# Tile 7's depthwise taps for both token chunks on TensorE, and one modulation section moved from TensorE to VectorE

## The chip, the cores and the metric

The kernel runs on one core of a Trainium2 chip. The metric is device microseconds of one execution. Before the change the median of three runs is 1677.97 us (1677.6 to 1678.09).

## The reference

A trunk of two layers over 1024 tokens of 1024 channels. Each layer is RMSNorm, shift and scale from a conditioning vector, a token mixer, a gated residual add, and then the same with a SwiGLU feed-forward part. The change concerns the first layer: its mixer (`conformer_conv`) and its modulation vector.

```python
def reference(x, c, ...):
    c_act = jax.nn.silu(c)
    for i in range(DEPTH):
        mod = c_act @ ada_w[i] + ada_b[i]
        sh_m, sc_m, g_m, sh_f, sc_f, g_f = jnp.split(mod, N_ADA, axis=-1)
        h = modulate(rms_norm(x, norm_mix_g[i]), sh_m, sc_m)
        ...
        x = x + (1.0 + g_m)[:, None, :] * y
        h = modulate(rms_norm(x, norm_ffn_g[i]), sh_f, sc_f)
        y = swiglu_ffn(h, ffn_w_gate[i], ffn_w_up[i], ffn_w_down[i])
        x = x + (1.0 + g_f)[:, None, :] * y

def conformer_conv(h, w1, b1, w_dw, b_dw, ln_g, ln_b, w2, b2):
    u = h @ w1 + b1
    a, g = jnp.split(u, 2, axis=-1)
    u = a * jax.nn.sigmoid(g)
    u = lax.conv_general_dilated(u, w_dw[:, None, :], ...,     # causal, depthwise,
        padding=[(CONV_WIDTH - 1, 0)], ...) + b_dw             # CONV_WIDTH = 31 taps
    u = jax.nn.silu(layer_norm(u, ln_g, ln_b))
    return u @ w2 + b2
```

## The kernel before

Channels lie on the 128 partitions in 8 tiles (0 to 7), tokens on the free axis in two chunks of 512, called A and B. Engines are named PE (TensorE), DVE (VectorE), ACT (ScalarE), POOL (GpSimd) and SP (SyncE) as in the profile. float32 products are made of three matmuls of split operands (high by high, high by low, low by high; `products`): a weight `w` has a high and a low part, and so have the activations. Low parts of weights are made by DVE, or by a DMA that adds the raw weight onto the negated high part (issued by POOL, `w<-in_..._dram`).

The instruction stream is written by a planner. Work for PE stands in a list of units; between matmuls `pace()` lets a set of tasks (generators) issue a step for DVE, ACT or POOL when the planner's clocks say so. A task that reaches a `yield "name"` is held for the time that the table `DELAY` gives that name. So the costs and delays, not the code's order alone, set where a vector instruction or a small matmul stands on its engine. Each engine then runs its instructions in the order written.

The stages that matter here, in order of PE's work in the first layer:

- `conv_in`: for each chunk and tile, 24 matmuls into bank `a` and 24 into bank `g` (weights w1, inputs `h`); `conv_glu` then makes u = (a + b1) * sigmoid(g + b1) on ACT and DVE. A rim of 30 tokens (`uhalo`) carries A's last tokens over to B.
- The 31 taps of the convolution. For most tiles class `Taps` makes them: DVE steps `ca<-u,vecs,ca` (a scalar times a shifted u plus a running sum, 128x512), and for a part of the taps ACT products `pr` that POOL adds up (`pa<-pa,pr`); then `ca<-pa,ca` joins the two and `u<-u,vecs,ca` ends the tile. For A's tile 6 (15 taps) and A's tile 7 (all 31) PE makes taps: `pe_taps` multiplies shifted windows of u (high and low part, `us`) by diagonal 128x128 matrices of tap weights (`wdg`), and the bank `tap` collects them. Tile 7 of A is 31 taps by 3 matmuls, with 512 columns at the first tap and down to 482 at the last.
- `layer_norm_silu(A)`: DVE adds the eight tiles into `acc`, a matmul with `ones` makes the mean (`mean<-acc,ones`), DVE subtracts it (`u<-u,mean`), then come squares, `var<-ones,acc`, `rstd<-ident,col`, and the normalised values `v`. PE fills the time with `conv_in` of B's tiles 3, 4 and 5.
- `conv_out(A)`: eight output tiles `y<-v,w` of 24 matmuls; then the last `conv_in` of B (tile 5), beside which the feed-forward norm of A (`norm_a`: `var`, `rstd`) runs; then the feed-forward part for A (`p<-h,w` for gate and up, `dn<-g,w` for down), beside which DVE and POOL finish B's taps and `layer_norm_silu(B)` runs.

The modulation vector has six sections of 1024 numbers (j = 0 to 5). In the first layer j = 0 and 1 are made by DVE dot products (`ada_dot`: weights `adaw` times the activated c, with the sum written to `mod`). j = 2 to 5 are made by PE in `ada_columns`: 32 matmuls `ada<-adaw,ccols` of 32 by 256 for a section, issued in pairs of two k (8 matmuls), then two `adac<-quarters,t` and a DVE add `mod<-adac,vecs`. j = 5 is the gate of the feed-forward residual, used first when A's `dn` ends. The weights `adaw` come through SP's queue into two buffers.

Of the kernel before, what the change touches and what calls it, by code (L numbers as in the profile page):

```python
# [133 lines left out]
def trunk(ctx, tc, xT, c, vec, ada, adan, w1f, w1, wdg, w2, wgu, wdn, wds, wpl, out):  # L134
# [267 lines left out]
    def ada_task(l, js, pause=None, first=None):  # L402

        def gen():
            todo = [(j, k) for j in js for k in range(KT)]
            ws = [ada_load(ada[(l * 6 + j) * KT + k], soft) for j, k in todo[:ADA_BUFS]]
# [333 lines left out]
    def conv_glu(ch, p, ba, bg, own=False):  # L740
# [5 lines left out]
        if ch.i == 0 and PE_TAPS.get(p) == CW:  # L746

            V_.scalar_tensor_tensor(ba, ba, V("conv_b1", p), sg, op0=ADD, op1=MUL)
            pair = wpair(B, "us", F32R)
            hi, lo = st["us", p] = [pair[:, i, : ch.width] for i in range(2)]  # L750
            for part in (hi, lo):
                G_.memset(part[:, HALO - 2 : HALO].bitcast(F32), 0.0)
            S_.copy(hi[:, HALO:], ba)
            V_.tensor_tensor(lo[:, HALO:], ba, hi[:, HALO:].bitcast(F32), op=SUB)
            S_.copy(uhalo[:, p, :], ba[:, ch.n - HALO :])
            return
# [42 lines left out]
    def pe_taps(p):  # L799
# [4 lines left out]
        for i, js in enumerate(groups):  # L804
            def emit(take, i=i, js=js):
# [3 lines left out]
                for q, j in enumerate(js):  # L809
                    full = PE_TAPS[p] == CW  # L810
                    o = (CW - 1 - j) // 2 * 2 if full else CW - 3 - j
                    c = j + o if full else 0
                    products(b[:, o:], wt, q, [v[:, c : c + A.n - o] for v in st["us", p]], j == groups[0][0], j == groups[-1][-1])
                    if q % 4 == 3:
                        pace()
                if i == len(groups) - 1:
                    if full:
                        S_.activation(st["u", 0, p][:, HALO:], b, AF.Identity, bias=V("conv_bdw", p))
                        st["taps", 0][p] = True
                    else:  # L820
                        T["taps", 0, p].other = b
# [1435 lines left out]
```

## Time and profile before

| | |
|---|---|
| median of three runs | 1677.97 us |
| profiled execution | 1675.66 us, span 1673.9 us, granted clock 0.998 |
| PE busy | 1651.8 us, 99% of the span |
| DVE busy | 1310.0 us, 78% |
| ACT busy | 804.1 us, 48% |
| POOL busy | 487.4 us, 29% |

The span is the time from the first to the last instruction of the profiled execution; 1.8 us lie around it. PE's share of 99% is one over the whole program. In the table below, of stretches in us from the span's start, the columns are the time and the number of instructions in which each engine was busy (PEld is the loading of weights, which overlaps PE), PE's granted clock, the mean share of the 16 DMA engines and GB/s. The change touches the first four stretches.

```profile
60.00:180.00 120.00, 119.71 (x610) 89.84 (x610) 107.87 (x169) 96.16 (x138) 90.41 (x84) 1.00 0.78 225
180.00:240.00 60.00, 60.00 (x306) 47.65 (x305) 52.17 (x86) 45.71 (x62) 43.76 (x41) 1.00 0.91 228
240.00:320.00 80.00, 79.95 (x415) 62.70 (x414) 72.90 (x115) 63.03 (x89) 59.71 (x53) 1.00 0.79 213
320.00:420.00 100.00, 98.69 (x433) 80.17 (x432) 90.88 (x120) 70.40 (x103) 80.54 (x61) 1.00 0.59 174
420.00:1674.00 1254.00, 1244.80 (x5607) 1033.39 (x5605) 933.02 (x1298) 505.68 (x671) 189.53 (x286) 1.00 0.74 228
```

### The profile page before, as it was taken

The page shows a single profiled execution, that of the slowest core. Times are in us where ns is not written, and L with a number is a line of the kernel's source. Part 1 is how long each engine was busy: PE and PEld are TensorE (multiplying, and loading weights), DVE is VectorE, ACT ScalarE, POOL GpSimd, SP SyncE. Part 2 cuts the span into 40 slices and gives each one's busy share as a digit, 9 for nine tenths or more (in the row PEclk, how much of TensorE's full clock was granted, in tenths as well). Part 3 has the DMA queues.
Part 4 walks back from the last instruction along what each step waited for, and adds up shares of the span by engine and source line. Part 5 has one row for each costly group of instructions (what it writes and reads, how often), then busy time and mean ns, then how long its engine had stood idle before and what let it go on. Part 6 is the DMA issues. An engine that isn't in the chain of part 4 may idle for free.

```text
span 1673.9 us, 21194 instructions
## 1 busy us (share of the span) xinstructions
PE 1651.8 (99%) x7550; PEld 1351.2 (81%) x7550; DVE 1310.0 (78%) x1867; ACT 804.1 (48%) x1090; POOL 487.4 (29%) x567
## 2 busy tenths in 40 slices
PE   7999999999999999999999999999999999999997
PEld 5777878787888888888888888888888888888887
DVE  8889899799759888888678957848777766658657
ACT  3669696867546332332234436637322222244354
POOL 3587777796002111221100502101111111000013
PEclk9999999999999999999999999999999999999999
DMA  8958997828776888886965959866777776686664
GB/s 301 295 176 228 225 236 205 226 78 241 229 234 168 278 264 287 282 272 206 400 231 164 285 155 283 247 211 199 189 225 222 220 227 183 207 273 207 192 170 126
DMA packets 117180, 378.60 MB, mean 226 GB/s; under 512 B 12369, under 2 KB 14545, under 8 KB 117074
## 3 DMA queue, kind: packets, MB, share of 16 engines
q1 hardware_dynamic: 79664, 245.63, 41.6%
q0 software_dynamic: 36832, 131.09, 32.5%
q8 instruction: 59, 0.97, 0.2%
q10 hardware_dynamic: 578, 0.53, 0.1%
q14 instruction: 47, 0.39, 0.1%
HBM read 310.61 MB, written 62.39 MB: 223 GB/s over the span
## 4 chain that ended last, share of the span: by engine, by line
PE 88%; POOL 3%; DVE 2%; DMA 2%; issue 2%; ACT 2%; DVEq 0%; SPq 0%; POOLq 0%; ACTq 0%
PE a L151 24%; PE dn L151 23%; PE e L151 14%; PE p L151 10%; PE y L151 6%; POOL pa L128 3%; PE first L151 3%; PE g L151 2%; PE tap L151 2%; DMA adaw<-in_adan_dram 1%; DMA s<-in_wds_dram 1%; PE ada L151 1%; ACT w L128 1%; DMA w<-in_wgu_dram 1%; PE var L151 1%
## 5 line engine op out<-in xcount | busy, mean ns | idle before, releaser
L128 ACT CAST w<-raw 128x1024 fp32r<-128x1024 f32 (+1 forms) x247 | 254.6, 1033 | 305.5 <-PE dn L151 56.9
L128 DVE TENSOR_TENSOR w<-raw,w 128x1024 fp32r<-128x1024 f32 (+1 forms) x173 | 209.3, 1214 | 62.2 <-ACT w L128 61.9
L151 PE MATMUL a<-n,w 128*128 128x512 f32 x1056 | 246.8, 389 | 0.2
L151 PE MATMUL p<-h,w 128*128 128x512 f32 x1056 | 243.7, 390 | 1.2 <-DMA w<-in_wgu_dram 1.0
L128 POOL TENSOR_TENSOR pa<-pa,pr 128x512 f32<-128x512 f32 x159 | 225.3, 1500 | 29.0 <-ACT pr L128 23.7
L151 PEld LDWEIGHTS p<-h,w 128*128 128x128 f32 x1056 | 197.3, 188 | 43.7 <-DMA w<-in_wgu_dram 1.4
L151 PEld LDWEIGHTS a<-n,w 128*128 128x128 f32 x1056 | 198.0, 188 | 42.2 <-DVE r L128 1.1
L151 PE MATMUL dn<-hi,w 128*128 128x512 f32 (+1 forms) x768 | 226.2, 377 | 0.4 <-DVE w L128 0.4
L151 PE MATMUL dn<-g,w 128*128 128x512 f32 x864 | 199.1, 390 | 0.2 <-DVE x L128 0.2
L151 PEld LDWEIGHTS dn<-g,w 128*128 128x128 f32 x864 | 161.7, 188 | 34.7 <-DVE x L128 0.6
L128 DVE SCALAR_TENSOR_TENSOR ca<-u,vecs,ca 128x512 f32<-128x512 f32 x246 | 170.6, 747 | 0.5
L151 PEld LDWEIGHTS dn<-hi,w 128*128 128x128 f32 x768 | 141.2, 188 | 27.0 <-DVE w L128 0.9
L151 PE MATMUL dn<-lo,w 128*128 128x512 f32 (+1 forms) x384 | 144.3, 376 | 0.0
L151 PE MATMUL a<-t,w 128*128 128x512 f32 x528 | 123.3, 389 | 0.0
L151 PE MATMUL e<-t,w 128*128 128x512 f32 x528 | 123.3, 389 | 0.0
L151 PE MATMUL e<-b,w 128*128 128x512 f32 x528 | 123.3, 389 | 0.0
L128 ACT ACTIVATE pr<-u,vecs 128x512 f32<-128x512 f32 x159 | 108.4, 717 | 25.0 <-POOL pa L128 19.7
L151 PEld LDWEIGHTS a<-t,w 128*128 128x128 f32 x528 | 99.1, 188 | 20.7
L151 PEld LDWEIGHTS e<-t,w 128*128 128x128 f32 x528 | 99.1, 188 | 20.6
L151 PEld LDWEIGHTS e<-b,w 128*128 128x128 f32 x528 | 99.1, 188 | 20.6
L1191 POOL DMA_DIRECT2D raw<-in_wgu_dram x41 | 36.5, 889 | 271.5 <-DVE r L128 104.2
L128 ACT CAST hi<-op 128x1024 fp32r<-128x1024 f32 (+1 forms) x52 | 48.5, 935 | 87.1 <-PE dn L151 77.2
(191 smaller groups left out, 2449.4 us busy)
## 6 DMA issues: line engine op xcount, KB each, us to landing
raw<-in_wgu_dram SPq DMA_DIRECT2D x132, 512.0 KB, 4.7
raw<-in_wds_dram SPq DMA_DIRECT2D x48, 512.0 KB, 6.0
adaw<-in_ada_dram POOLq DMA_DIRECT2D x48, 512.0 KB, 6.8
kinds<-k POOLq DMA_DIRECT2D x42, 512.0 KB, 7.7
raw<-in_wgu_dram POOLq DMA_DIRECT2D x41, 512.0 KB, 7.3
raw<-in_w_dram SPq DMA_DIRECT2D x36, 512.0 KB, 6.6
op<-kinds SPq DMA_DIRECT2D x36, 512.0 KB, 4.8
adaw<-in_adan_dram SPq DMA_DIRECT2D x32, 512.0 KB, 5.5
```

What stands on the lines that cost most here:

```text
L128: self.last = self.order(getattr(self.eng, name)(out, *args, **kw))
L151: last_mm[0] = nc.tensor.matmul(out, lhsT, rhs, start=start, stop=stop, skip_group_check=more).ins.name
L1191: d = order(nc.gpsimd.dma_start(w[i], wgu[l, fp, src], accum_op=ADD))
```

## The change

1. Tile 7's taps are made on PE for both chunks. Tokens are split into even and odd ones (two phases, f), and the 128 rows of a matrix are 2 phases by 64 channels, for each half g of the tile's channels. A matmul then carries 512 columns: 256 token pairs of A beside 256 of B. 31 taps become 16 pair shifts m, so that 2 halves by 16 shifts by 3 products give 96 matmuls of 512 columns, with matrices that couple the two phases (`dense`), in place of 93 for A alone. `halves` makes the operands (four DVE steps of 64x256 for each chunk, a high copy on ACT and a low part on DVE), and ACT brings the result back in eight pieces of 64x256. DVE's and POOL's 31 taps for B's tile 7 are gone.
2. j = 5 of the first layer is made by `ada_task` on DVE (eight dot products of 128x1024, sum and gain on POOL) in place of `ada_columns`. Its weights come through SP's queue as before, from another array; it is created after j = 4 is done (`scale_done`) and ended in `first_head`.
3. `conv_out(A)` makes its output tiles 0 and 1 in turn (k by k), as B's did.
4. The mean of A's layer norm is delayed by 4.6 of the planner's us ("mean") in place of 2.75 ("stats").

```diff
-DELAY = {"stats": 2.75, "spread": 3.0, ...
+DELAY = {"mean": 4.6, "stats": 2.75, "spread": 3.0, ...
-    def ada_task(l, js, pause=None, first=None):
+    def ada_task(l, js, pause=None, first=None, queue=soft):
...
+        if PE_TAPS.get(p) == CW:
+            return u
...
+    def halves(ch, p, ba, sg):
+
+        n = ch.n // 2
+        t = temp(ch.n).rearrange("p (g n) -> p g n", g=2)
+        for g in range(2):
+            at = slice(HALF * g, HALF * g + HALF)
+            for f in range(2):
+                V_.scalar_tensor_tensor(t[HALF * f : HALF * f + HALF, g], ba[at].rearrange("p (n f) -> p f n", f=2)[:, f], V("conv_b1", p)[at],
+                                        sg[at].rearrange("p (n f) -> p f n", f=2)[:, f], op0=ADD, op1=MUL)
...
+        S_.copy(hi, t)
+        V_.tensor_tensor(lo, t, hi.bitcast(F32), op=SUB)
+
+    def pe_halves(p):
+
+        blocks = [(g, m) for g in range(2) for m in range(NM)]
...
+                    products(b, wt, q, [part[:, g, m : m + 512] for part in st["us", p]], m == 0, m == NM - 1)
...
+                            for f in range(2):
+                                at = slice(HALF * f, HALF * f + HALF)
+                                S_.activation(d[:, f], b[at, n * ch.i : n * ch.i + n], AF.Identity, bias=V("bdw_halves", g)[at])
...
-        yield "soon" if ch.i else "stats"
+        yield "soon" if ch.i else "mean"
...
-        for ds in [(0, 1) if ch.i else (0,), *(() if ch.i else ((1,),)), *((d,) for d in range(2, KT))]:
+        for ds in [(0, 1), *((d,) for d in range(2, KT))]:
...
-        for u in pe_taps(p):
+        for u in pe_halves(p) if PE_TAPS[p] == CW else pe_taps(p):
             unit(*u)
...
-        T["ada_f"] = Task(ada_columns((4, 5)), False, 0)
+        T["ada_f"] = Task(ada_columns((4,)), False, 0)
...
-    taps(B, *some, *rest[: len(rest) - HOLD - HOLD_LN])
+    taps(B, *[p for p in some if PE_TAPS.get(p, 0) < CW], *rest[: len(rest) - HOLD - HOLD_LN])
...
     unit(scale_done)
+    unit(lambda take: T.__setitem__("ada_g", ada_task(0, (5,), "load", queue=sync)))
...
-        unit(lambda take: finish(T["ada_f"]))
+        unit(lambda take: finish(T["ada_g"]))
```

How the order changes, at three places. Rows are instructions in the order of an engine, with the numbers of the tiles; "x3" is three in a row.

First place: DVE between the add `mod<-adac,vecs` of section j = 3 (it waits for two small matmuls of PE that stand behind the first 12 tap matmuls of tile 7) and the first `ca<-pa,ca` behind it; both kernels then go on to the last add of A's `acc`, which the mean waits for. Before:

```order
L128 TENSOR_TENSOR mod<-adac_1792,vecs 128x8
L128 SCALAR_TENSOR_TENSOR ca_1559<-u_721,vecs,ca_1559 128x512
L128 SCALAR_TENSOR_TENSOR ca_1591<-u_721,vecs,ca_1591 128x512
...
L128 TENSOR_TENSOR ca_1559<-pa_1529,ca_1559 128x512
L128 SCALAR_TENSOR_TENSOR ca_1591<-u_721,vecs,ca_1591 128x512
L128 SCALAR_TENSOR_TENSOR u_721<-u_721,vecs,ca_1559 128x512
```

After:

```order
L130 TENSOR_TENSOR mod<-adac_1796,vecs 128x8
L130 SCALAR_TENSOR_TENSOR ca_1622<-u_721,vecs,ca_1622 128x512
L130 SCALAR_TENSOR_TENSOR ca_1566<-u_721,vecs,ca_1566 128x512
...
L130 TENSOR_TENSOR ca_1566<-pa_1556,ca_1566 128x512
L130 SCALAR_TENSOR_TENSOR ca_1622<-u_721,vecs,ca_1622 128x512
L130 SCALAR_TENSOR_TENSOR u_721<-u_721,vecs,ca_1566 128x512
```

The rows left out are `ca` steps of the same two running sums: between `mod` and the first `ca<-pa,ca` stand 6 of them before and 17 after. Up to the mean's last `acc` it is 33 DVE instructions before and 41 after, the difference being 8 `ca` steps.

Second place: PE at the end of the tap matmuls. Before:

```order
L151 MATMUL tap_1779<-us_1229,w_1735 128x484 x6
L151 MATMUL tap_1779<-us_1229,w_1735 128x482 x3
L151 MATMUL a_1975<-h_801,w_1769 128x512 x3
...
L151 MATMUL a_1975<-h_808,w_1769 128x512 x3
L151 MATMUL mean_2010<-acc_1962,ones 128x512
L151 MATMUL g_1976<-h_801,w_1829 128x512 x3
```

After:

```order
L153 MATMUL tap_1889<-us_1233,w_1742 128x512
L153 MATMUL tap_1889<-us_1232,w_1742 128x512
L153 MATMUL a_1996<-h_801,w_1776 128x512 x3
...
L153 MATMUL a_1996<-h_808,w_1776 128x512 x3
L153 MATMUL mean_2031<-acc_1983,ones 128x512
L153 MATMUL g_1997<-h_801,w_1834 128x512 x3
```

The mean stands behind the same 24 matmuls of `conv_in` as before; the taps ahead of it are 512 wide throughout.

Third place: PE around the mean of B's layer norm, in the feed-forward part. Before:

```order
L151 MATMUL dn_3976<-g_3744,w_3796 128x512 x3
L151 MATMUL dn_3977<-g_3744,w_3796 128x512 x3
L151 MATMUL mean_3990<-acc_3961,ones 128x512
L151 MATMUL dn_3974<-g_3843,w_3848 128x512 x3
L151 MATMUL dn_3975<-g_3843,w_3848 128x512 x3
```

After:

```order
L153 MATMUL p_3718<-h_2812,w_3663 128x512 x3
L153 MATMUL p_3718<-h_2813,w_3663 128x512 x3
L153 MATMUL mean_3861<-acc_3841,ones 128x512
L153 MATMUL p_3719<-h_2810,w_3663 128x512 x3
L153 MATMUL p_3719<-h_2811,w_3663 128x512 x3
```

Before, the mean stands behind 12 matmuls of the down projection; after, it stands 36 matmuls ahead of that projection's start, which is 48 matmuls earlier. From B's layer norm on, the order of all engines soon becomes the same in both kernels.

More of the change, by code (lines that the diff above doesn't have):

```diff
@@ L104, in tap_groups @@
     n = PE_TAPS[p]
-    todo = list(range(CW - 1, -1, -1) if n == CW else range(CW - 3, CW - 3 - 2 * n, -2))
+    todo = list(range(CW - 3, CW - 3 - 2 * n, -2))
     return [todo[i : i + DIAGS] for i in range(0, len(todo), DIAGS)]
@@ L400, in ada_load @@
         return w
[L402 removed]
+    def ada_task(l, js, pause=None, first=None, queue=soft):
         def gen():
             todo = [(j, k) for j in js for k in range(KT)]
[L406 removed]
+            ws = [ada_load(ada[(l * 6 + j) * KT + k], queue) for j, k in todo[:ADA_BUFS]]
             for i, (j, k) in enumerate(todo):
@@ L411, in gen @@
                     j2, k2 = todo[i + ADA_BUFS]
-                    ws.append(ada_load(ada[(l * 6 + j2) * KT + k2], soft))
+                    ws.append(ada_load(ada[(l * 6 + j2) * KT + k2], queue))
                 if k == KT - 1:
@@ L745, in conv_glu @@
             tc.add_manual_dep(S_.last.ins, st.pop("v_high"), edge, reason="behind the layer norm's last high part")
[L746 to L755, printed above, removed]
+        if PE_TAPS.get(p) == CW:
+            halves(ch, p, ba, sg)
             return
@@ L809, in emit @@
                 for q, j in enumerate(js):
[L810 to L813, printed above, removed]
+                    o = CW - 3 - j
+                    products(b[:, o:], wt, q, [v[:, : A.n - o] for v in st["us", p]], j == groups[0][0], j == groups[-1][-1])
                     if q % 4 == 3:
@@ L816, in emit @@
                 if i == len(groups) - 1:
[L817 to L821, printed above, removed]
+                    T["taps", 0, p].other = b
             us.append((emit, wdg[sum(len(tap_groups(q)) for q in PE_TAPS if q < p) + i]))
@@ L2207 @@
         ada_b, norm_mix_g, norm_ffn_g, conv_b1, conv_bdw, conv_ln_g, conv_ln_b, conv_b2, c, pool_ls, final_g, conv_wdw)])
+    whole = [p for p in PE_TAPS if PE_TAPS[p] == CW]
+    vec = np.concatenate([vec, np.tile(np.asarray(conv_bdw).reshape(KT, 2, HALF)[whole].reshape(-1, HALF), (1, 2))])
     def tiles(w, f):
@@ L2219 @@
     taps = np.asarray(conv_wdw)[0].reshape(CW, KT, P)
-    groups = [(p, js) for p in sorted(PE_TAPS) for js in tap_groups(p)]
+    groups = [(p, js) for p in sorted(PE_TAPS) if PE_TAPS[p] < CW for js in tap_groups(p)]
     diag = np.zeros((len(groups), P, DIAGS, P), np.float32)
@@ L2224 @@
             diag[i, range(P), q, range(P)] = taps[j, p]
+    dense = np.zeros((len(whole), 2, NM, 2, HALF, 2, HALF), np.float32)
+    for i, p in enumerate(whole):
+        for m in range(NM):
+            for f in range(2):
+                for o in range(2):
+                    j = 2 * (m - LEAD) + CW - 1 + f - o
+                    if 0 <= j < CW:
+                        dense[i, :, m, f, range(HALF), o, range(HALF)] = taps[j, p].reshape(2, HALF).T
+    dense = dense.reshape(-1, DIAGS, P, P).transpose(0, 2, 1, 3)
+    diag = np.concatenate([diag, dense])
     down = np.asarray(ffn_w_down).reshape(DEPTH, NP, 2, P, 2, D // 2)
```

32 lines of the change are left out of this document (29 added, 3 removed).

## The prediction

> **What bounds the kernel now.** I read the busy times first, then the chain that ended last, then what TensorE (PE) waited for, and then the timeline of PE and DVE in the stretches that the change touches.
>
> From the page: busy times, and shares of the chain by engine.
>
> ```profile
> PE 1651.8 (99%) x7550; PEld 1351.2 (81%) x7550; DVE 1310.0 (78%) x1867; ACT 804.1 (48%) x1090; POOL 487.4 (29%) x567
> PE 88%; POOL 3%; DVE 2%; DMA 2%; issue 2%; ACT 2%; DVEq 0%; SPq 0%; POOLq 0%; ACTq 0%
> ```
>
> PE's waits (line, releaser: total us, times, longest):
>
> ```profile
> PE var L151 <- DVE acc L128: 4.9, 1, 4.9
> ...
> PE p L151 <- DMA w<-in_wgu_dram: 1.0, 1, 1.0
> ```
>
> PE is busy for 99% of the span and carries 88% of the chain. The largest wait, 4.9 us, belongs to the first norm of the program. In the stretches of the change only the 1.0 us for `w<-in_wgu_dram` is a wait of size. So the time is PE's instructions plus whatever waits appear: a matmul taken away counts fully, DVE and POOL work counts only where PE comes to need it. The question is how near DVE already is to PE there.
>
> PE at tile 7's taps (start us, us, form, count with the weight loads of a merged row counted apart):
>
> ```profile
> 175.68 5.64 PE L151 MATMUL tap<-us,w 128*128 128x490 f32 x24
> 181.16 0.51 PE L151 MATMUL adac<-quarters,t 128*128 128x4 f32 x4
> 181.52 18.61 PE L151 MATMUL tap<-us,w 128*128 128x508 f32 x81
> 199.97 5.62 PE L151 MATMUL a<-h,w 128*128 128x512 f32 x24
> 205.43 1.02 PE L151 MATMUL mean<-acc,ones 128*128 128x512 f32 x2
> ```
>
> DVE in the same stretch (the bracket is idle time before, and what ended it):
>
> ```profile
> 181.70 0.17 DVE L128 TENSOR_TENSOR mod<-adac,vecs 128x8 f32<-128x8 f32 x1 [1.65 <-PE adac L151]
> 181.78 4.30 DVE L128 SCALAR_TENSOR_TENSOR ca<-u,vecs,ca 128x512 f32<-128x512 f32 x6
> 186.28 0.70 DVE L128 TENSOR_TENSOR ca<-pa,ca 128x512 f32<-128x512 f32 x1 [0.19 <-POOL pa L128]
> ...
> 190.18 5.35 DVE L128 SCALAR_TENSOR_TENSOR ca<-u,vecs,ca 128x512 f32<-128x512 f32 x8
> ...
> 203.35 1.50 DVE L128 TENSOR_TENSOR acc<-acc,u 128x512 f32<-128x512 f32 x2
> 208.14 2.48 DVE L128 TENSOR_TENSOR u<-u,mean 128x512 f32<-128x512 f32 x4 [3.29 <-ACT ny L128]
> ```
>
> What to see: the last `acc` ends at 203.35 + 1.50 = 204.85, and PE takes it for the mean at 205.43. The margin is 0.58 us. And DVE's run up to it begins at a fixed point: the add `mod` waits (1.65 us of idle) for two small matmuls of PE inside the taps.
>
> **Part 1: taps on PE.** 93 matmuls become 96. The 81 from 181.52 to 199.97 took 18.45 us, 228 ns each at about 495 columns; the 24 of 512 columns behind them took 205.43 - 199.97 = 5.46 us, also 228 ns. If columns don't count, the price is 3 x 0.228 = +0.7 us. If time goes with columns, it is 93 x 0.228 x (96 x 512 / (93 x 497) - 1) = +1.3 us (497 is the mean of 512 to 482). I take +1.1 and keep both ends.
>
> [...]
>
> The new high copies, low parts and 16 evictions of 64x256 lie on ACT and DVE beside taps and `conv_in`; they cost nothing as long as DVE's 1.65 us of idle before `mod` covers them. The order places B's four 64x256 steps and the low part some 30 rows before `mod`. If that cover fails, the excess adds to part 3's wait.
>
> **Part 2: section j = 5 off PE.** Rows around its last two places, in the feed-forward part:
>
> ```profile
> 299.89 4.92 PE L151 MATMUL p<-h,w 128*128 128x512 f32 x21
> 304.74 1.07 PE L151 MATMUL ada<-adaw,ccols 128*32 128x256 f32 x16
> 305.74 11.90 PE L151 MATMUL p<-h,w 128*128 128x512 f32 x51
> 317.56 1.07 PE L151 MATMUL ada<-adaw,ccols 128*32 128x256 f32 x16
> 318.56 5.78 PE L151 MATMUL p<-h,w 128*128 128x512 f32 x24
> 324.18 0.50 PE L151 MATMUL adac<-quarters,t 128*128 128x4 f32 x4
> 324.54 20.65 PE L151 MATMUL p<-h,w 128*128 128x512 f32 x90
> ```
>
> From 299.89 to 324.18 are 24.29 us with 96 `p` matmuls; 96 x 0.228 = 21.89, which leaves 2.40 for two pairs, 1.20 each. `adac` takes 324.54 - 324.18 = 0.36. Four pairs and the `adac`: -5.2 us. None of it hid anything on PE, so all of it counts until a wait gives it back.
>
> On DVE the eight dots (price in part 5) go where B's tile-7 taps were. Their loads are eight of 512 KB on SP's queue as before, but each now waits for a DVE dot instead of a PE pair, ahead of raw weights of the feed-forward part. Cover: those raw weights are taken by ACT casts ahead of PE's use. I cost it at nothing, between -0.3 (smoother) and +1 (as much as PE's one wait for a weight there now).
>
> **Part 3: a new wait at the mean of A's layer norm.** In the new order 8 more `ca` steps stand between `mod` and the last `acc` (41 DVE instructions, 33 before), and `mod` still waits for the same place among the taps. 8 `ca` steps took 5.35 us (190.18), so `acc` ends at 204.85 + 5.35 - 0.19 (the wait for POOL's `pa`, whose sum is then eleven steps older) = 210.0. PE gets to the mean at 205.43 + 1.1 = 206.5. New wait: +3.5 us. The bounds: 0, should DVE do without the wait at `mod`, and 5.35, all eight steps bare. I stay near the worked value, because `mod` and all that follow it stand in one queue that runs in order. What is queued behind PE's wait is 24 `g` matmuls and everything after; the whole rest of the program moves. It gives back two thirds of part 2. The planner's longer delay for this mean doesn't help: the order puts it behind the same 24 matmuls.
>
> **Part 4: the first two output tiles, interleaved.**
>
> ```profile
> 238.91 11.58 PE L151 MATMUL y<-v,w 128*128 128x512 f32 x48
> 250.41 1.07 PE L151 MATMUL ada<-adaw,ccols 128*32 128x256 f32 x16
> 251.41 10.76 PE L151 MATMUL y<-v,w 128*128 128x512 f32 x46
> ```
>
> The first 48 take 250.41 - 238.91 = 11.50 us against 48 x 0.228 = 10.94. The 0.56 holds a stall as `v` comes in; with two tiles in turn each `v` is needed half as fast. I take -0.3 (0 to -0.5).
>
> **Part 5: the feed-forward part.** POOL and PE at the 1.0 us wait (POOL first):
>
> ```profile
> 365.35 9.26 POOL L128 TENSOR_TENSOR pa<-pa,pr 128x512 f32<-128x512 f32 x6
> 374.60 1.13 POOL L128 TENSOR_SCALAR pa<-u,vecs 128x512 f32<-128x512 f32 x1
> 375.70 1.30 POOL L128 TENSOR_TENSOR pa<-pa,pr 128x512 f32<-128x512 f32 x1
> 376.92 0.91 POOL L506 DMA_DIRECT2D w<-in_wgu_dram  x1
> ```
>
> ```profile
> 386.81 27.04 PE L151 MATMUL p<-h,w 128*128 128x512 f32 x118 [1.01 <-DMA w<-in_wgu_dram]
> 413.69 2.88 PE L151 MATMUL dn<-g,w 128*128 128x512 f32 x12
> 416.66 1.10 PE L151 MATMUL mean<-acc,ones 128*128 128x512 f32 x2
> ```
>
> The DMA that adds a low part is issued behind POOL's `pa` adds, at 376.92, and PE needs it about 385.8. PE will be some 1 us earlier, POOL has one tile's adds fewer but the rest re-packed. Between -1.0 (the wait goes) and +1.7 (POOL a `pa` add late); I take 0.
>
> DVE at the mean of B's layer norm, and two groups (count, busy us, mean ns):
>
> ```profile
> 404.45 2.09 DVE L128 TENSOR_TENSOR w<-raw,w 128x1024 fp32r<-128x1024 f32 x1 [2.47 <-ACT w L128]
> ...
> 414.09 1.22 DVE L128 TENSOR_TENSOR w<-raw,w 128x1024 fp32r<-128x1024 f32 x1
> 415.23 0.68 DVE L128 TENSOR_TENSOR g<-ny,g 128x512 fp32r<-128x512 f32 x1
> 415.83 0.69 DVE L128 TENSOR_TENSOR acc<-acc,u 128x512 f32<-128x512 f32 x1
> ```
>
> ```profile
> L128 DVE SCALAR_TENSOR_TENSOR ca<-u,vecs,ca 128x512 f32<-128x512 f32 x246 | 170.6, 747 | 0.5
> L128 DVE SCALAR_TENSOR_TENSOR adaw<-adaw,cact 128x1024 f32<-128x1024 f32 x64 | 77.5, 1215 | 0.7 <-DMA adaw<-in_ada_dram 0.7
> ```
>
> The last `acc` ended at 415.83 + 0.69 = 416.52, PE's mean began at 416.66: no margin. In the new order that matmul stands 48 matmuls earlier, 48 x 0.228 = 10.9 us, and PE is 1.0 ahead: needed at 404.7. DVE does between the two means 25 fewer tap instructions (22 `ca`) at about 0.67, 16.8 us, and eight dots more at 1.215 + 0.08, 10.4 us: 6.4 earlier. The rest comes from feed-forward work that then stands behind the mean (from 404.45 on three `w<-raw,w`, 2.09 + 2 x 1.22, and three of 0.68: 6.6 us): 416.5 - 6.4 - 6.6 = 403.5, 1.2 us in time, and 2.47 us of idle beside it. I take 0.
>
> **Sum.** +1.1 - 5.2 + 3.5 - 0.3 + 0 + 0 = -0.9 us. The profiled execution took 1675.66 us (span 1673.9 and 1.8 around it), 2.3 below the median of 1677.97; the difference carries over: 1674.8 profiled, 1677.1 as a median. That is -0.05%, inside the 0.2% (3.4 us) that a measurement of this kernel can tell from no change.
>
> **The rivals.**
> - No wait at A's mean: DVE reaches `mod` at the same moment but loses nothing, because the planner's order is not what runs last (for example `ca` steps faster without POOL beside them). -0.9 - 3.5 = -4.4: 1673.6, faster. For it: before, DVE and PE met here within 0.58. Against it: eight steps of a row-proven 0.67 and a queue in order.
> - B's mean late: if the 6.6 us of feed-forward work on DVE doesn't fall behind the mean, the last `acc` comes at 410.1 against 404.7, PE waits 5.4 us: -0.9 + 5.4 = +4.5: 1682.5, slower. It decides from 4.3 us of lateness on. For it: no margin at 416.66 now. Against it: DVE idles (2.47) in that stretch.
> [...]
> - The saving is eaten whole by small waits (SP's queue, part 2): 1678.
>
> **How the numbers follow.** Chances: the forecast 0.42, no wait at A's mean 0.21, B's mean late 0.20, POOL freed 0.12, eaten whole 0.05. Faster by over 0.2% (below 1674.6): most of the second and the low ends of the others, 0.26. Slower (above 1681.3): 0.14 of the third, since it may be late by less, and 0.04 from high ends of parts 2, 3 and 5, 0.18. Same: 0.56. The range goes from 1672.6, the first rival with its parts at their low ends, to 1682.0, just short of the late mean's full price; beyond each lies about 0.1. The forecast alone would span 1675 to 1680.
>
> **What would show it.** Right: PE's waits list a `mean` for DVE's `acc` of 2.5 to 4.5 us once; PE has 32 `ada` matmuls fewer; 96 `tap` matmuls of tile 7 in 21.9 to 22.5 us; no wait at the second `mean`. Wrong: no such wait (then faster), a second `mean` wait of several us, or waits for `w<-raw` or `p` that SP's or POOL's queue brings.

## The result, and the profile after: 1.6% slower

| | before | after |
|---|---|---|
| time, median | 1678.03 us | 1704.67 us |
| lowest to highest | 1677.6 to 1679.56 | 1703.6 to 1707.01 |
| ratio after/before | | 1.0159 (95% interval 1.0141 to 1.0177) |
| profiled execution | 1675.66 us, span 1673.9 | 1704.12 us, span 1702.3 |
| PE's mean granted clock | 0.998 | 0.991 |

The forecast was 1677.1 us, in a range of 1672.6 to 1682.0. The change costs 26.6 us. The busy times and the chain of after:

```profile
PE 1658.0 (97%) x7485; PEld 1356.3 (80%) x7485; DVE 1321.8 (78%) x1863; ACT 804.8 (47%) x1091; POOL 486.3 (29%) x560
PE 83%; ACT 5%; DMA 4%; DVE 3%; POOL 3%; issue 2%; SPq 0%; DVEq 0%; POOLq 0%; ACTq 0%
```

PE has 65 instructions fewer (64 `ada` and 4 `adac` out, 3 taps in), and is yet busy 6.2 us longer. Its share of the span falls from 99% to 97%. Both say the same: PE stands still where it did not, and runs slower behind it. PE's waits (total us, times, longest):

```profile
PE var L153 <- DVE acc L130: 6.0, 1, 6.0
PE dn L153 <- DVE ny L130: 6.0, 1, 6.0
PE y L153 <- ACT t L130: 4.6, 1, 4.6
PE y L153 <- DMA w<-in_w_dram: 4.4, 2, 2.9
PE mean L153 <- DVE acc L130: 3.6, 2, 3.0
...
PE a L153 <- ACT t L130: 2.2, 2, 1.1
```

Only the first of these was there before (4.9 us). The timeline of PE, from the taps to the first output tiles, in the feed-forward part, and at B's output projection (start, us, what, count, and in brackets the idle time before):

```profile
185.90 19.80 PE L153 MATMUL tap<-us,w 128*128 128x512 f32 x84
205.53 5.64 PE L153 MATMUL a<-h,w 128*128 128x512 f32 x24
214.21 1.10 PE L153 MATMUL mean<-acc,ones 128*128 128x512 f32 x2 [3.03 <-DVE acc L130]
214.74 7.66 PE L153 MATMUL g<-h,w 128*128 128x512 f32 x24
```

```profile
254.96 12.82 PE L153 MATMUL y<-v,w 128*128 128x512 f32 x45 [4.58 <-ACT t L130]
```

```profile
367.51 22.39 PE L153 MATMUL dn<-g,w 128*128 128x512 f32 x87 [6.01 <-DVE ny L130]
```

```profile
476.64 43.55 PE L153 MATMUL y<-v,w 128*128 128x512 f32 x180 [2.88 <-DMA w<-in_w_dram]
```

What to see: the mean's wait is the one that was forecast (3.03 us for 3.5). The three others were not. And the 24 `g` behind the mean took 7.66 us, where 24 `a` just ahead took 5.64. The granted clock says why; stretches of after (busy us and counts of PE, PEld, DVE, ACT and POOL, then PE's clock, DMA share, GB/s), at the mean's wait and at that of `dn`:

```profile
212.20:215.60 3.40, 1.39 (x5) 0.86 (x5) 1.72 (x3) 1.27 (x3) 0.86 (x1) 1.00 0.95 177
215.60:219.00 3.40, 3.40 (x10) 2.66 (x9) 3.04 (x6) 2.62 (x5) 2.99 (x3) 0.50 1.04 249
219.00:222.40 3.40, 3.40 (x19) 2.52 (x21) 2.98 (x6) 2.53 (x5) 0.21 (x1) 1.00 0.48 94
```

```profile
365.80:369.20 3.40, 1.69 (x4) 1.40 (x5) 3.40 (x5) 1.71 (x3) 2.76 (x2) 0.50 0.51 154
369.20:372.60 3.40, 3.40 (x9) 2.63 (x9) 2.80 (x5) 0.71 (x3) 2.87 (x3) 0.50 0.26 67
```

The clock is halved for 3.4 us behind the mean's wait, and for 6.8 us at each of the three others (253.2 to 260.0, 365.8 to 372.6, 475.0 to 481.8), of which the wait itself covers a part. Then it is 1.00 again. 3.4 us at half clock cost a busy PE 1.7. The ledger of the span, +28.4 us: all PE waits that the view lists sum to 37.5 us against 15.3 (+22.2); PE's instructions at full clock are -5.2 + 1.1 = -4.1; the rest, 10.3, is put down to the slower clock behind the waits. Four runs hold 9.3 of it: `g` 7.66 - 6.02 (its time before) = 1.6, and 45 `y`, 87 `dn` and 180 `y`, each its time less its count at 0.228: 2.6, 2.6 and 2.5.

The experiments are read by one table: how much later than in the kernel before PE starts an instruction, in us, from the two timelines.

| PE starts | after | e1 | e16 | e17 | e18 | e3 | e12 | e13 |
|---|---|---|---|---|---|---|---|---|
| the first tap | 4.4 | 4.5 | 4.4 | 3.7 | 3.7 | 6.2 | 3.7 | 1.1 |
| the last tap | 5.6 | 5.7 | 5.6 | 4.9 | 4.8 | 7.4 | 4.8 | 2.3 |
| A's mean | 8.8 | 8.9 | 8.8 | 8.1 | 8.4 | 10.6 | 8.1 | 3.5 |
| A's first `y` | 10.5 | 10.6 | 10.5 | 9.8 | 10.1 | 12.3 | 9.8 | 3.6 |
| A's last `y` | 16.0 | 9.9 | 9.8 | 9.0 | 9.4 | 12.9 | 10.3 | 4.1 |
| the first `dn` | 12.9 | 7.0 | 6.9 | 6.2 | 5.9 | 12.9 | 10.3 | 4.3 |
| B's first `y` | 20.7 | 16.6 | 15.9 | 9.1 | 8.8 | 19.5 | 10.1 | 4.2 |
| B's last `y` | 28.2 | 29.3 | 15.9 | 9.1 | 8.8 | 19.5 | 10.1 | 4.2 |
| PE's last instruction | 28.4 | 30.2 | 16.2 | 9.7 | 8.8 | 19.7 | 10.1 | 4.3 |

### The profile page after: what moved, and what is told of

Same layout as the page of the kernel before. It is cut to its first block, busy times and chain, and to the rows that moved or that the text cites. A ratio compares the mean times of both kernels' runs of the same rounds, so it can differ in the third digit from the quotient of the medians.

```text
span 1702.3 us, 21045 instructions
## 1 busy us (share of the span) xinstructions
PE 1658.0 (97%) x7485; PEld 1356.3 (80%) x7485; DVE 1321.8 (78%) x1863; ACT 804.8 (47%) x1091; POOL 486.3 (29%) x560
## 4 chain that ended last, share of the span: by engine, by line
PE 83%; ACT 5%; DMA 4%; DVE 3%; POOL 3%; issue 2%; SPq 0%; DVEq 0%; POOLq 0%; ACTq 0%
PE dn L153 23%; PE a L153 23%; PE e L153 14%; PE p L153 9%; PE y L153 7%; PE first L153 3%; POOL pa L130 2%; DMA adaw<-in_adan_dram 2%; PE g L153 2%; ACT w L130 2%; PE tap L153 1%; ACT pr L130 1%; DVE ca L130 1%; DMA raw<-in_wdn_dram 1%; DMA w<-in_w_dram 1%
## 5 line engine op out<-in xcount | busy, mean ns | idle before, releaser
L130 DVE SCALAR_TENSOR_TENSOR ca<-u,vecs,ca 128x512 f32<-128x512 f32 x223 | 155.0, 746 | 0.6
L130 ACT ACTIVATE pr<-u,vecs 128x512 f32<-128x512 f32 x154 | 105.2, 716 | 29.3 <-POOL pa L130 19.4
L153 PE MATMUL y<-v,w 128*128 128x512 f32 x384 | 93.7, 406 | 9.0 <-ACT t L130 4.6
```

The lines of the kernel that those rows point to most:

```text
L130: self.last = self.order(getattr(self.eng, name)(out, *args, **kw))
L153: last_mm[0] = nc.tensor.matmul(out, lhsT, rhs, start=start, stop=stop, skip_group_check=more).ins.name
```

## The experiments

Ratios are to the kernel before on the same chip, with 95% intervals; its median lies between 1676.5 and 1678.0 in all of them. The parts are numbered as in the change: 1 taps, 2 j = 5, 3 in turn, 4 delay.

### The parts alone: e5, e4, e3

**e5_in_turn**: the kernel before with part 3 alone.

```diff
-        for ds in [(0, 1) if ch.i else (0,), *(() if ch.i else ((1,),)), *((d,) for d in range(2, KT))]:
+        for ds in [(0, 1), *((d,) for d in range(2, KT))]:
```

> The kernel before with one part of the change alone: A's output tiles 0 and 1 in turn. Theory 1 (the second bank that two tiles in turn need is held by ACT's sigmoid, which stands behind the layer norm's work): y waits 4 to 5 us at about 239 us and 2 us more go to the lower clock: 1676.5 + 6.5 = 1683. Theory 2 (PE makes this up later, as the kernel without this part was no faster than the changed one): within 0.2% of before, 1675 to 1680 us.

1687.85 us, ratio 1.0065 (1.005 to 1.008). Its new wait of PE:

```profile
PE y L151 <- ACT t L128: 4.0, 1, 4.0
```

What ACT does at that moment in after:

```profile
252.29 0.62 ACT L130 CAST v<-t 128x512 fp32r<-128x512 f32 x1
252.93 1.28 ACT L130 ACT_TABLE_LOAD   x1
254.22 0.69 ACT L130 ACTIVATE t<-g,vecs 128x512 f32<-128x512 f32 x1
```

The second of two tiles in turn needs a second PSUM bank at once. PE waits there for ACT's `t`, which reads the last `g` of `conv_in` out of its bank. ACT reads it in `t<-g`, which stands behind the layer norm's `v` and a table load: it starts at 254.22, PE goes on at 254.96. So interleaving alone is dear: a wait of 4.0 us, further waits later (2.2 us at B's mean, 1.5 at a `p`), and 2.8 us that are no wait and are put down to the clock (the span is 11.0 us longer, all listed waits together 8.2).

**e4_dots**: the kernel before with part 2 alone.

```diff
-        T["ada_f"] = Task(ada_columns((4, 5)), False, 0)
+        T["ada_f"] = Task(ada_columns((4,)), False, 0)
...
     unit(scale_done)
+    unit(lambda take: T.__setitem__("ada_g", ada_task(0, (5,), "load", queue=sync)))
...
-        unit(lambda take: finish(T["ada_f"]))
+        unit(lambda take: finish(T["ada_g"]))
```

> The kernel before with section j = 5 moved to VectorE alone; taps, output tiles and delay as before. Theory 1: PE saves 5.2 us, and gets a wait at the feed-forward part's dn or at B's mean of up to 6 us with 2.6 us of slow matmuls: 1677 to 1682 us. Theory 2 (the dots hurt only together with the new taps): 1672.8 us.

1694.47 us, ratio 1.0101 (1.0084 to 1.0118). The 5.2 us that leave PE come back with 18 more: waits at `dn`, `p`, `y` (two) and B's `rstd`. In its order B's `rstd` stands 4 matmuls ahead of B's first `y`, where it was 58 before.

**e3_taps_delay**: the kernel before with parts 1 and 4. (The delay alone leaves every engine's order in the kernel before as it was.) The diff is that of the change without the lines of parts 2 and 3.

> The kernel before with tile 7's taps on TensorE for both chunks and the new delay of A's mean alone (no tiles in turn, no dots). Theory 1: what is left of the loss is 3.7 us of waits ahead of the taps, the mean's wait of 3.0 with 1.7 of slow matmuls behind it, 1.1 of more tap matmuls, and 0 to 7 for the y of chunk B (not yet put down to a part): 1678 + 9.5 = 1687.5, up to 1694.5. Theory 2: 1700 or more.

1695.76 us, ratio 1.0103 (1.0083 to 1.0123). The `mean` waits 3.0 us here too, so that wait is of the taps, not of the dots or the interleaving. A new one stands ahead of B's `y`:

```profile
464.96 4.61 PE L153 MATMUL p<-h,w 128*128 128x512 f32 x12 [4.24 <-ACT r L130]
```

Alone the parts cost 11, 18 and 19 us, 48 in all; together 26.6. They don't add: the waits of one part cover or move those of another, as e1 shows next.

### Parts taken out of after: e1, e2

**e1_apart**: after without part 3 (e5's diff reversed).

> The changed kernel with one part undone: A's output tiles 0 and 1 stand one behind the other again (y of tile 0, then y of tile 1). Changed kernel 1704.7 us. Theory 1 (each new wait has its own part of the change, and a wait of 3 us or more costs about 2 us more through the lower clock behind it): the 4.6 us wait of y for ACT's t belongs to this part, since two tiles in turn need a second bank that ACT's sigmoid still holds; it goes, with 2.4 us of slow matmuls behind it, so 1697.7 us. Theory 2 (any edit redraws the planner's whole order, and new waits come wherever PE is ahead): the wait is replaced by another within 20 us, 1702 to 1708 us.

1706.04 us, ratio 1.0167 (1.015 to 1.0184): no faster. The wait at A's `y` went, and A's last `y` comes 6.2 us earlier. All of it is lost at B's `y`:

```profile
PE y L153 <- DMA w<-in_w_dram: 10.3, 2, 6.2
```

There is also a new wait of 3.9 us at a `p` for DVE's `w`. In after, PE comes to B's `y` 4 us later than here, and the last of these weights lands 2 us earlier (476.6 against 478.8 us; the rows are at e16 below).

**e2_j5_pe**: after without part 2 (e4's diff reversed).

> The changed kernel with one part undone: section j = 5 by TensorE again. Theory 1: the 6.0 us wait of dn for DVE's ny at 361 us belongs to the eight dots on DVE (two of them, 1.7 and 2.3 us, stand ahead of ny there); it goes with 2.6 us of slow matmuls behind it, and PE gets 5.2 us of matmuls back: 1704.7 - 8.6 + 5.2 = 1701.3 us. Theory 2: DVE is late there because of the tap steps in their new order; the wait stays, 1707 to 1710 us.

1699.26 us, ratio 1.0132 (1.0114 to 1.0149). Some 5 us faster than after: the 6.0 us wait at `dn` is gone, and a wait of 4.3 at a `p` before B's `y` has come, the one of e3. So with all else in place the dots cost 5 us, where -5.2 was forecast.

### Is it DVE's time on the dots, or their loads? e7 to e10

**e7_dots_short** and **e8_after_dots_short**: the dots of j = 5 on 8 columns in e4 and in after, the planner charged for all. **e9_dots_no_load** and **e10_after_dots_no_load**: their loads cut to n = 8 columns too.

```diff
-        V_.scalar_tensor_tensor(w, w, 1.0, cact, op0=MUL, op1=MUL, accum_out=mod[:, b : b + 1])
+        if (l, j) == (0, 5):
...
+            V_.last = order(nc.vector.scalar_tensor_tensor(w[:, :8], w[:, :8], 1.0, cact[:, :8], op0=MUL, op1=MUL, accum_out=mod[:, b : b + 1]))
+            return
...
-        queue.dma_start(w, src)
+        queue.dma_start(w[:, :n], src[:, :n])
```

> The kernel with section j = 5 moved to VectorE alone (1694.5 us), with each of the eight dots cut to 8 of its 1024 columns, and the planner charged as for the whole; loads, queues and the order of every engine as there. It leaves out all but 64 of the 8192 products of each of the section's numbers. Theory 1 (the dots' time on DVE, about 10 us or more, is what PE waits for later): PE's 5.2 us come out, 1671 to 1674 us. Theory 2 (the new order, SP's loads and POOL's sums do it): 1688 or more.

> The changed kernel (1704.7 us) with its eight dots cut to 8 of 1024 columns in the same way, order unchanged. It leaves out the same products. Theory 1: the wait of dn for ny (6.0 us and 2.6 of slow matmuls) goes: 1696 us, and up to 7 us less if the late y of chunk B hangs on it too, 1689. Theory 2: 1702 to 1706 us.

> As the kernel with section j = 5 moved to VectorE alone and its dots cut to 8 columns (1691.5 us), and now their loads cut to 8 of 1024 columns too, so that neither DVE time nor DMA bytes of the section are left; the order of every engine as there. It leaves out the same products. Theory A (eight loads of 512 KB meet the feed-forward weights in a stretch where the DMA engines are full): 1672 to 1680. Theory B (the written order itself: in it, rstd of B's layer norm stands 4 matmuls ahead of B's first y, 58 before): 1686 or more.

> The changed kernel with dots and their loads cut in the same way, order unchanged (with the dots alone cut: 1703.4 us). It leaves out the same products. Theory A: 1690 to 1696. Theory B: 1700 to 1704.

1691.51 (ratio 1.0082, 1.0064 to 1.01), 1703.38 (1.0157, 1.014 to 1.0174), 1694.05 (1.0095, 1.0078 to 1.0112) and 1703.3 us (1.0151, 1.0136 to 1.0166). PE's order stayed as it was; on the other engines a few dozen rows changed places, so these are not quite the kernels they were cut from. Against e4 and after the time falls by 3.0, 1.3, 0.4 and 1.4 us. The loads are no cause, and the dots' own time is a small part there. In e8 the wait at `dn` falls from 6.0 to 1.9, and the time doesn't follow: it is taken up at B's mean (2.5 for `ny`) and at B's `y` (5.1 for `w`). What is left is the order. That was tested next.

### The place of B's layer norm: e12, e16

**e12_taps_mean_b_late** is e3, and **e16_placed** is e1, with a delay of its own for the mean of B's layer norm: 20 and 8 of the planner's us (and the same entry in the second table of delays, `DELAY_BEHIND`).

```diff
-        yield "soon" if ch.i else "mean"
+        yield "mean_b" if ch.i else "mean"
...
-DELAY = {"mean": 4.6, "stats": 2.75, ...
+DELAY = {"mean": 4.6, "mean_b": 8, "stats": 2.75, ...
```

> The kernel with taps and A's delay alone (1695.8 us), with a delay of 20 of the planner's us for the mean of B's layer norm, which puts it 153 matmuls ahead of B's first y (249 without, 141 in the kernel before). Theory A (there B's layer norm ends early, and its weights' casts and loads come too late against the other transfers, so that p waits 4.2 us for ACT's r at 461 us): that wait and its 2.2 us of slow matmuls go, 1689.5. Theory B (the transfers are late whatever the mean does): 1694 to 1697.

> The same without moving the bias adds. Theory A: 1686.5 - 5.2 = 1681.3. Theory B: 1688 to 1698.

e12: 1686.51 us, ratio 1.0054 (1.0039 to 1.0069), 9.3 us below e3; by the table 2.6 of that (6.23 - 3.67) lie ahead of the taps, where the order is the same and e3 met a slow stretch (last section), so some 7 are the delay's. e16: 1690.43 us, ratio 1.0078 (1.0063 to 1.0093), 15.6 us below e1, by a single number; up to A's last `y` the two run alike. In e12 that mean stands 153 matmuls ahead of B's first `y`, in e16 141, as many as in the kernel before; in e3 249, in e1 177. In e12 the 4.24 us at `p` is gone, in e16 the 10.3 us at `y`. PE at B's `y`, in e1:

```profile
471.20 1.42 PE L153 MATMUL y<-v,w 128*128 128x512 f32 x3 [4.05 <-DMA w<-in_w_dram]
478.84 41.33 PE L153 MATMUL y<-v,w 128*128 128x512 f32 x175 [6.22 <-DMA w<-in_w_dram]
```

and in e16:

```profile
465.84 43.68 PE L153 MATMUL y<-v,w 128*128 128x512 f32 x192
```

Between e1 and e16 this is the largest cost that one placement shows. The mean itself is cheap where it stands early (0.6 us of wait in after and in e1). What costs is what the order then puts behind it. PE's two waits at `y` in e1 are for the low parts of the first weights, two transfers that POOL issues (`w<-in_w_dram`). POOL in e1 (the last line is the time of these two transfers from issue to landing):

```profile
456.71 0.88 POOL L1226 DMA_DIRECT2D raw<-in_wgu_dram  x1 [40.66 <-ACT w L130]
457.35 1.14 POOL L508 DMA_DIRECT2D w<-in_w_dram  x1
459.69 0.86 POOL L1226 DMA_DIRECT2D raw<-in_wgu_dram  x1 [1.20 <-DMA raw<-in_wgu_dram]
467.69 0.88 POOL L508 DMA_DIRECT2D w<-in_w_dram  x1 [7.15 <-ACT v L130]
DMA to landing us min/median/max: 11.1/12.5/13.8
```

and in e16:

```profile
453.44 0.89 POOL L508 DMA_DIRECT2D w<-in_w_dram  x1 [37.35 <-PE rstd L153]
455.34 0.86 POOL L508 DMA_DIRECT2D w<-in_w_dram  x1 [1.01 <-ACT w L130]
467.80 0.87 POOL L1226 DMA_DIRECT2D raw<-in_wgu_dram  x1 [11.61 <-ACT v L130]
```

In e1 they land at 457.35 + 13.8 = 471.15 and 467.69 + 11.1 = 478.79, and PE goes on at 471.20 and 478.84. In e16 both are issued over 10 us ahead of B's first `y` (465.84). In e1 the first is 9.2 us ahead of it (466.53) and the second 1.2 us behind it, because it stands behind a second `raw` load in POOL's order and then waits for ACT's `v`. ACT is late too in e1. It stands idle for 9.97 us at a step of the layer norm, with the casts `w<-raw` behind it:

```profile
449.96 0.82 ACT L130 ACTIVATE t<-u,vecs 128x512 f32<-128x512 f32 x1 [9.97 <-DVE u L130]
```

In e16 five instructions that make `w` from `raw` run ahead of that step. After has the same lateness as e1: its two transfers are issued at 459.90 and 463.33, take 12.8 to 13.3 us, and its waits at `y` end at 472.79 and 476.64. That these two issues hold `y` up is read from the traces. No run moves them alone, and none moves B's mean in after itself.

### The wait at A's mean: e6, e11, e13, e14

**e6_hold** and **e11_hold_long**: the kernel before with 5 and 9 needless DVE steps (`acc` times 1) ahead of A's mean.

```diff
+        if ch.i == 0:
+            for _ in range(5):      # e11: 9
+                order(nc.vector.tensor_scalar(acc, acc, 1.0, None, op0=MUL))
         yield "soon" if ch.i else "stats"
```

> The kernel before with five needless steps on DVE (acc times 1.0, 128x512, chained) ahead of the mean of A's layer norm, order on all other engines unchanged. It makes PE wait there for 5 x 0.7 - 0.6 = 2.9 us. Theory 1 (a wait of about 3 us lowers PE's granted clock for the matmuls behind it): +2.9 + 1.7 = 4.6 us, 1681.1. Theory 2 (only the wait counts): 1679.4. Theory 3 (later waits shrink by as much): 1676.5.

> The kernel before with nine needless DVE steps ahead of the mean of A's layer norm, where five made PE wait 1.7 us and cost 3.4 us in all with PE's clock at 1.00. Nine give a wait of 1.7 + 4 x 0.45 = 3.5 us. If a wait of 3 us or more lowers the granted clock behind it and one of 1.7 doesn't: 24 g matmuls take 7.6 us in place of 6.0 and the time is 1677.1 + 3.4 + 1.8 + 1.7 = 1684.0. If the clock stays: 1682.3.

e6: 1680.59 us, ratio 1.0019 (1.0009 to 1.0028). e11: 1683.37 us, ratio 1.0035 (1.0023 to 1.0046). In e6 the wait came out at 1.71 us and not at the 2.9 expected; the four steps more of e11 added 0.47 each (3.57 - 1.71 over four). PE in e6, and PE and a stretch of it in e11:

```profile
208.20 1.10 PE L151 MATMUL mean<-acc,ones 128*128 128x512 f32 x2 [1.71 <-DVE acc L928]
208.73 6.03 PE L151 MATMUL g<-h,w 128*128 128x512 f32 x24
```

```profile
210.14 1.35 PE L151 MATMUL mean<-acc,ones 128*128 128x512 f32 x2 [3.57 <-DVE acc L928]
210.68 7.65 PE L151 MATMUL g<-h,w 128*128 128x512 f32 x24
```

```profile
210.00:218.00 8.00, 7.86 (x26) 5.80 (x26) 5.53 (x9) 4.76 (x8) 3.27 (x4) 0.79 0.64 148
```

From the mean to A's first `y` e6 loses nothing more (2.8 us late at the one, 2.9 at the other), e11 1.7 (4.7 and 6.4): 24 `g` in 7.65 us, where e6 has 6.03. The 0.79 is an average over 8 us; with the 0.50 of after it stands for an estimated 3.4 us of slow clock (8 x 0.21 / 0.50). In e6 the clock was 1.00 from 208 to 216. The two kernels differ in the length of this wait alone, so the drop belongs to the longer idle.

**e13_bias_a** is e12 with A's eight bias adds (`x` + `gate_b`, ACT) held behind the split of B's tile 7; **e14_bias_ab** holds all sixteen.

```diff
             S_.activation(x[ch.i][k], x[ch.i][k], AF.Identity, bias=gate_b[:, k : k + 1])
+            if ch.i == 0:           # e14: for both chunks
+                tc.add_manual_dep(S_.last.ins, st["halves"], edge, reason="behind the halves")
```

> The kernel with taps, A's delay and B's mean late (1686.5 us), with chunk A's eight bias adds (ACT, x + gate_b, 128x512) held until B's tile 7 is split. In its order mod stands 8 ca steps earlier again, as in the kernel before. Theory A (ACT's backlog of bias adds is what put 8 more ca steps behind mod and so made the mean wait): the wait of 3.0 us and 1.7 of slow matmuls go, 1681.8. Theory B (DVE has more to do ahead of the mean with the new halves, wherever mod stands): 1685 to 1687.

> The same with all sixteen bias adds held, so that none stands ahead of the sigmoid that two a waits of 1.1 us hang on. Theory A: these go too, 1679.6. Theory B: 1684 or more.

e13: 1682.06 us, ratio 1.0029 (1.0019 to 1.0039), 4.4 below e12. The two `a` waits of 1.1 are gone, 21 `ca` steps stand behind `mod` as before the change (29 in after), and the mean's wait shrinks:

```profile
208.90 1.10 PE L153 MATMUL mean<-acc,ones 128*128 128x512 f32 x2 [1.01 <-DVE acc L130]
```

So the wait that was forecast has its root one step further back, in ACT's queue: the bias adds that come to stand among the copies and evictions of the new taps. e14 goes too far: 1684.09 us, ratio 1.004 (1.0025 to 1.0055), with a new wait of 3.0 us at a `tap` for ACT.

### What the dots cost in their place: e15, e17, e18

**e15_all_placed** is e16 with all sixteen bias adds held (e14's edit).

> The changed kernel with tiles 0 and 1 one behind the other, B's mean later (141 matmuls ahead of B's first y, as in the kernel before) and all sixteen bias adds held. Theory A (placed so, taps and dots cost what their instructions cost): 1677.1 + 1.1 - 5.2 + 1 = 1674. Theory B (DVE, POOL and ACT can't carry the dots in the feed-forward part wherever things stand): PE waits there of 5 to 10 us, 1682 to 1690.

1687.88 us, ratio 1.0063 (1.0048 to 1.0078). With the dots e16 and e15 are 3.9 and 3.8 us above the kernels with j = 5 on PE (e12, e14), which differ from them also in the delay of B's mean, 20 in place of 8. Two waits in the feed-forward part make it; e16's rows:

```profile
PE p L153 <- DVE w L130: 4.0, 1, 4.0
...
PE dn L153 <- DVE ny L130: 2.5, 1, 2.5
```

DVE at the first of them, and POOL beside it:

```profile
384.12 5.56 DVE L130 TENSOR_TENSOR w<-raw,w 128x1024 fp32r<-128x1024 f32 x1 [1.70 <-ACT w L130]
```

```profile
367.45 21.13 POOL L130 TENSOR_TENSOR pa<-pa,pr 128x512 f32<-128x512 f32 x16
```

A subtraction that took 1.22 to 2.09 us in the rows of before took 5.56, and ended 1.1 us after POOL's run of 16 adds did (367.45 + 21.13 = 388.58). That looks like waiting for the adds and not like work. e17 tests it, and e18 the dots' own share.

**e17_placed_adds_short**: e16 with those 16 adds on 8 columns. **e18_placed_dots_short**: e16 with the dots on 8 columns (e7's edit).

```diff
-                    G_.tensor_tensor(self.part, self.part, pr, op=ADD)
+                    if ch.i == 1 and (p == 3 and 10 <= self.ng <= 16 or p == 4 and 5 <= self.ng <= 13):
...
+                        G_.last = order(nc.gpsimd.tensor_tensor(self.part[:, :8], self.part[:, :8], pr[:, :8], op=ADD))
+                    else:
+                        G_.tensor_tensor(self.part, self.part, pr, op=ADD)
```

> e16 with 16 of POOL's `pa` adds of B's tap tiles 3 and 4 (the run of 16 that took 21.13 us up to 388.5 in e16) working on 8 columns in place of 512; the planner is charged for the full width, so PE's and DVE's orders stay. What is left out: those products are missing from B's taps. In e16 PE waits 3.99 us at a `p` of the feed-forward part for a DVE `w<-raw,w` that took 5.56 us, from 384.12 to 389.7, while POOL's adds ran back to back at 1.25 us each; the same form takes 1.2 us where POOL is idle. Theory (contention): POOL's adds hold DVE's subtraction back, both reading two operands from SBUF. Then the subtraction takes 1.2 to 1.5 us, PE's wait for `w` is under 0.3 us, its slow clock behind it (0.66 over 8 us in e16) is gone, and the time falls by 4 to 7 us, from 1690.4 to 1683.5 to 1686.5. Rival (the subtraction is slow for another reason, its own operands or the load beside it): it takes 5 us again and the time stays within 1.5 us of 1690.4.

> e16 with the eight dots of section j = 5 working on 8 columns in place of 1024; the planner is charged for the full width, and PE's order stays. What is left out: most of that section's sums. In e16 PE waits 2.48 us at `dn` for DVE's `ny`; between 341 and 358 three dots stand on DVE at 1.73, 2.25 and 1.21 us. Theory A (the `dn` wait is DVE's own time on the dots): three dots shorter by some 1.0 to 2.1 us each, the wait is gone and its slow clock with it, the time falls by 2.5 to 4.5 us, to 1686 to 1688; the 3.99 us wait at `p` stays or moves by under 1 us. Rival B (the wait comes from the order, where `ny` stands behind split and tap work): the wait stays above 1.5 us and the time within 1.5 us of 1690.4. Rival C (POOL's adds fill the freed time and come to stand elsewhere): the `dn` wait goes but the `p` wait changes by over 1 us.

e17: 1686.28 us, ratio 1.0057 (1.0043 to 1.0071). PE's and DVE's orders are e16's. The subtraction:

```profile
381.63 2.17 DVE L130 TENSOR_TENSOR w<-raw,w 128x1024 fp32r<-128x1024 f32 x1
```

The wait at that `p` is gone, and 4.2 us with it: POOL's adds held the subtraction back (5.56 us beside the 16 at full width, 2.17 with them short). The subtraction took 2.17 us and not the 1.2 to 1.5 expected; one add of full width was left beside it (381.11 to 382.7), and it ended 1.1 us after that. e18: 1684.62 us, ratio 1.0045 (1.0033 to 1.0058), 5.8 below e16. Its `dn` runs through, and the long subtraction stays, earlier by what DVE is ahead:

```profile
352.24 21.96 PE L153 MATMUL dn<-g,w 128*128 128x512 f32 x96
```

```profile
377.80 5.55 DVE L130 TENSOR_TENSOR w<-raw,w 128x1024 fp32r<-128x1024 f32 x1 [1.59 <-ACT w L130]
```

```profile
359.99 22.27 POOL L130 TENSOR_TENSOR pa<-pa,pr 128x512 f32<-128x512 f32 x17
```

Again the subtraction ends (377.80 + 5.55 = 383.35) 1.1 us after the adds (359.99 + 22.27 = 382.26). So the dots cost twice: DVE's time on them holds `ny` back, and what DVE does next meets POOL's adds. No kernel tried is faster than the one before.

## Why the prediction was wrong, point by point

By the table, after loses 4.4 us ahead of the taps, 1.2 in them, 4.9 from there to A's first `y`, 5.5 in A's `y`, gains 3.1 up to the first `dn`, loses 7.8 from there to B's first `y` and 7.5 in B's `y`. The forecast had 0, 1.1, 3.5 and -0.3 for the first four, -5.2 for the dots in all, and 0 for the last two.

- **Part 1, +1.1 for the taps on PE: right.** From the first tap to the last, after is 5.56 - 4.40 = 1.16 us longer. The clause that the copies and evictions cost nothing beside it was wrong. It named the cover, DVE's 1.65 us of idle before `mod`, and not ACT's queue, where the cost is: 2.2 us of waits of `a` for ACT, and most of the mean's wait. e13, which moves eight ACT instructions, takes back 4.4 us. After is already 4.4 us late at the first tap: besides these two waits of `a`, `ada` waits 0.5 and 1.1 us more for its weights, and the first norm is 0.4 longer, which no run isolates.
- **Part 3, +3.5 for the wait at A's mean: right in place and size (3.03), short in price.** This wait of 3.03 us cost 1.7 more by the clock (8.8 us late at the mean, 10.5 at A's first `y`), so it comes to 4.7. The rival without this wait is out.
- **Part 2, -5.2: the step "all of it counts until a wait gives it back" failed.** Taken off PE it was, 68 instructions. But dots stand on DVE ahead of `ny` in the feed-forward part, and only SP's queue and the mean were looked at there. In after this is the 6.0 us at `dn`, which e2 removes together with the dots; the wait that POOL's adds cause comes out only where earlier waits are gone (3.9 us at `p` in e1). With B's mean placed as before, the dots lose 3.9 us net (e16 against e12) in place of gaining 5.2: a miss of 9.1. e18 and e17 give back 5.8 and 4.2 of it, each with its other part left in.
- **Part 5, 0 for B's mean: the step that failed most.** The working asked whether DVE's `acc` is in time for the mean, and it nearly is (0.6 us of wait). That agreement is partly luck: the mean stands at 425.87 us where 404.7 was worked out, PE and DVE being late together. It didn't ask what the rest of the layer norm, now 96 matmuls earlier in e3's order than in e12's and 36 in e1's than in e16's, pushes back. By e1 and e16 this is 15.6 us, by e3 and e12 about 7. In after itself only the 7.5 us in B's `y` can be read as its price; no run separates it there. The rival that named B's mean had the place but the wrong mechanism (a wait of 5.4 us at the mean itself).
- **Part 4, -0.3 for the tiles in turn: wrong in sign.** Whether the stall of 0.56 us goes can't be read beside the new wait; the second PSUM bank that two tiles need at once was not counted, nor ACT, which PE then waits for. 4.6 us of wait and 2.6 of clock in after. Undone in after it brings nothing (e1), since the weights of B's `y` then end the wait.
- **POOL freed**, with 0.12 of the chances: not seen. It needs `pa` adds that run shorter once tile 7's tap steps are off DVE, and no run shows that. The six adds in 9.26 us that part 5 shows, 1.54 each, are four of 1.29 to 1.31 us and two of 1.74 and 2.16, and tap steps stand beside the short ones too. `w<-in_wgu_dram` is no longer among PE's waits in after, but nothing is gained by it. What the runs showed is the other side: adds that hold DVE's subtraction back (5.56 us in e16, 2.17 in e17).
- **The range** took the changed order as a cost of one wait at a time. Four places were spoilt at once.

What stays open: which of the rows that move with B's mean makes POOL issue the two transfers for `y` late (read from the traces, not tested alone), what the place of that mean costs in after, and which of the many moved rows of e4 make its waits at `y`.

## What to carry to other kernels

Where the bound engine is busy for 99% and a planner redraws the order, the sum over added and removed instructions is the small part (here -4.1 of +28.4 us). Look, at each place that the order moves, for who feeds the bound engine next: the queue that frees its PSUM bank, the engine that splits its weights, the loads behind those, and whether a long chain such as a layer norm now stands ahead of them. Undo one placement at a time (one delay gave 15.6 us here), since parts that look harmful alone may be free in company, and the reverse.

## What the runs showed of the hardware

- **PE's clock after a short idle.** In after the clock fell to 0.50 for 3.4 us behind an idle of 3.03 us, and for 6.8 us at each of the idles of 2.88, 4.58 and 6.01, at 1.6 to 2.6 us each. In e11 it was 0.79 over 8 us behind 3.57, in e16 0.84 over 9 us behind 2.48 at `dn`, and in e6 1.00 behind 1.71. Between 30 and 1650 us of before and after it was 1.00 everywhere else, and every other idle of PE there was 1.53 us or shorter. In e3 the clock fell (0.77 over 7.4 us, 24 `a` in 7.33 us in place of 5.71) behind a wait of 1.0 and two thin runs of `ada` and one-column `var`:

```profile
91.47 0.64 PE L153 MATMUL ada<-adaw,ccols 128*32 128x256 f32 x8 [1.01 <-DMA adaw<-in_adan_dram]
92.04 1.05 PE L153 MATMUL var<-ones,acc 128*128 128x1 f32 x8
92.95 7.33 PE L153 MATMUL a<-h,w 128*128 128x512 f32 x24
```

At the same place, with the same thin runs, PE waited 0.79 us in after and kept its clock (24 `a` in 5.75 us), and so it did at its three waits of 1.06 to 1.09 us between 143 and 172 (1.00 from 140 to 175). So the length of the idle alone doesn't decide.
- **DVE held up by POOL.** A 128x1024 subtraction with both operands in SBUF took 5.55 us (e18) and 5.56 (e16) beside adds of POOL that followed one another without a gap, 2.17 with those adds cut (e17) and 1.22 in the rows of before. In the first three runs it ended 1.1 us after the last add of full width, as if it got no turn between adds: in e16 and e18 it ran 4.46 us beside them (384.12 to 388.58, and 377.80 to 382.26), which is over three adds of 1.3 each (21.13 us for 16). It isn't always DVE that waits: in before, one subtraction started at 397.55 as an add was ending (397.72) and took 1.25 us, and the next add took 2.17 in place of 1.30.
